# Strassen weight blocks formed by accumulating DMAs, with signs laid out so that they are only added

## The chip, the cores and the metric

One core of a Trainium2 chip runs the program. The metric is the device time of one execution in microseconds (us). The engines are TensorE (PE in the profile, with PEld for its weight loads), VectorE (DVE), ScalarE (ACT), GpSimd (POOL) and SyncE (SP, which here only issues DMAs).

## The reference

One layer of a streaming encoder, 512 tokens by a model width of 2048, all in float32. Nearly all arithmetic is in three projections; between them stand twelve heads of attention of three kinds.

```python
def hybrid_layer(x, norm_g, w_in, b_f, b_gate, qk_norm_g, rel_bias, w_up, w_out):
    hn = rmsnorm(x, norm_g)
    proj = jnp.einsum('bsd,dc->bsc', hn, w_in)          # 2048 -> q, k, v, g of 12 heads, 4 logits, 3 x 2048 gates
    ...
    ya = forgetting_attention(qa, ka, to_heads(br[:, :, 0, 2]), f_logit)
    yb = chunked_relpos_attention(qb, kb, to_heads(br[:, :, 1, 2]), rel_bias)
    yc = stick_breaking_attention(...)
    ys = jnp.stack([from_heads(ya), from_heads(yb), from_heads(yc)], axis=2)
    ys = ys * jax.nn.silu(br[:, :, :, 3])
    up = jnp.einsum('bsnw,nwd->bsnd', ys, w_up)
    merged = jnp.sum(gates * up, axis=2)
    return x + jnp.einsum('bsd,de->bse', merged, w_out)
```

## The kernel before

Tokens lie in the free dimension. A column tile is 128 columns of a weight matrix; its 2048 rows are two halves of 8 k tiles of 128. Each float32 operand is split into a high and a low float32r part (`split_to`: ScalarE writes the high part, VectorE subtracts it from the source, line 93), and `mm3` makes a product of three matmuls: high by high, low of x by high, high of x by low.

Column tiles go in pairs, and a pair is computed by Strassen's method in Winograd's form: the 2 x 2 blocks of the weights (column tile by half of the rows: a11, a12 of the first tile, a21, a22 of the second) and of x (half of the model width by half of the tokens) need seven products of 8 k tiles by 256 tokens in place of eight. Three of the seven stationary operands are blocks as they are (product 1: a11, product 2: a12, product 4: a22), the others are sums: product 5 takes a21 + a22, product 6 that sum less a11, product 7 a11 - a21, product 3 a12 less product 6's operand. `pair_task` makes the seven units of a pair, in the order 1, 2, 6, 7, 4, 5, 3 (for the first pair of the output projection, called late: 1, 2, 5, 3, 6, 7, 4). The sums of x's blocks are made once: `combos` for the input projection (GpSimd, lines 257 to 260, then splits on ScalarE and VectorE), `merged_combos` for the output projection.

Each unit has a load, a preparation (sums and split into `wh` and `wl`), matmuls and an evacuation. Raw weight tiles (`raw`, 512 KB each) rotate through six buffers, `wh` and `wl` through three each, PSUM tiles `acc` through four. All four blocks of a pair are loaded by the unit that comes first in it, on SyncE's queue. The four sums of a pair are VectorE operations on whole raw tiles (lines 315, 324, 325, 327). The loop at the end prepares two units ahead and loads up to seven ahead (`LA`, `LD`); the framework's scheduler then sets the order within each engine's queue, and every engine runs its queue in order. In the first units (`manual_schedule`) TensorE keeps the written order.

The program starts with 16 tiles of x, the first head's q, k, v, g projected from the unnormed x without Strassen's method, and `combos` of the normed x at the same time (`x` there holds x1 and x2, the two halves of the model width; `t` holds t23 and t4, the sums). Then come 46 pairs of the input projection with the attention of the heads between them, the up projections, and eight pairs of the output projection. In the accumulation of a pair's results, `u`, `c1` and `c2` are SBUF tiles that VectorE updates from PSUM after each product.

Of the kernel before, what the change touches and what calls it, by code (L numbers as in the profile page):

```python
# [15 lines left out]
P = 128  # L16
# [9 lines left out]
UK = 8  # L26
# [12 lines left out]
def hybrid_kernel(  # L39
# [60 lines left out]
    def mm3(ps, lh, ll, rh, rl, start, stop):  # L100
        nc.tensor.matmul(ps, lh, rh, start=start, stop=False)  # L101
        nc.tensor.matmul(ps, lh, rl, start=False, stop=False)  # L102
        nc.tensor.matmul(ps, ll, rh, start=False, stop=stop)  # L103

    # ------------------------------------------------------------------ constants
# [18 lines left out]
    class Unit:  # L124
        """A stretch of the tensor engine's work with one stationary operand of up to 8 k tiles."""

        def __init__(self, shape, prep, mms, srcs=(), after=None):
            self.shape, self.prep, self.mms, self.srcs, self.after = shape, prep, mms, srcs, after
            self.hi = self.lo = None
# [4 lines left out]
    def load(u):  # L134
        u.raw = []
        for s, keep in u.srcs:
            t = raw_tile(u.shape)
            nc.sync.dma_start(t, s)
            u.raw.append(t)
            if keep is not None:  # L140
                keep.append(t)
# [8 lines left out]
    def prep_raw(u):  # L150
        split_to(u.hi, u.lo, u.raw[0])
# [21 lines left out]
    # -1 where key k >= j: suffix sums inside a block  # L173
# [4 lines left out]
    # A, rows are queries: NEG where the key (free) is after the query  # L178
# [4 lines left out]
    # C, rows are keys: valid where the query (free) is after the key  # L183
# [7 lines left out]
    # column h has ones on the rows h, 32 + h, 64 + h, 96 + h  # L191
# [6 lines left out]
    # the query gains carry the softmax scale  # L198
# [33 lines left out]
    def rsqrt(y, ps, n):  # L232
        """y = (ps / n + EPS) ** -0.5: a guess by exp and ln, and one Newton step."""
# [64 lines left out]
    def pair_task(src1, src2, ops, done, late=False, before_last=None):  # L298
# [3 lines left out]
        kept = []  # L302
# [608 lines left out]
```

## Time and profile before

| | |
|---|---|
| runs | 1399.37, 1399.85, 1400.12 us (median 1399.85) |
| span of the profiled execution, first to last instruction | 1397.6 us |
| its own time | not listed apart; the runs lie 1.8 to 2.5 us above that span |
| TensorE busy | 1366.3 us, 98% |
| VectorE busy | 1191.8 us, 85% |
| ScalarE busy | 729.7 us, 52% |
| GpSimd busy | 53.7 us, 4% |
| DMA | 176.39 MB, mean 126 GB/s |

The columns of a group of instructions are: line, engine, operation, output and inputs by the program's names, shapes, count, busy us, mean ns of one, and the idle time just before them with what ended it. A row of the order of time has its start, its duration, the engine and line; in brackets stands the idle time ahead of it and who ended it. A row of a stretch has its limits, its length, the busy time (and count) of each engine, TensorE's granted clock as a share of full speed, the DMA engines' mean busy share and GB/s. A line L93 is the helper's, whoever calls it; the tile names tell the calls apart. Matmul rows overlap, since matmuls are pipelined.

### The profile page before, as it was taken

How to read it: one execution, taken by the hardware profiler on the slowest of the kernel's cores; microseconds unless marked ns; L12 is line 12 of the kernel's file. 1: busy time of each engine (PE TensorE's matmuls, PEld its weight loads, DVE VectorE, ACT ScalarE, POOL GpSimd, SP SyncE). 2: the span in 40 equal slices, each digit the busy share in tenths (PEclk: the TensorE clock that was granted, in tenths of full speed). 3: DMA queues.
4: the chain of work that ended last, by engine and by line, in shares of the span. 5: the costliest groups of instructions: out<-in, count | busy, mean ns of one | idle time of the engine just before them, and what ended most of it. 6: DMA issues, size and time to landing. Idle time of an engine off the chain costs nothing.

```text
span 1397.6 us, 25474 instructions
## 1 busy us (share of the span) xinstructions
PE 1366.3 (98%) x10452; PEld 1316.7 (94%) x10452; DVE 1191.8 (85%) x1671; ACT 729.7 (52%) x1042; POOL 53.7 (4%) x60
## 2 busy tenths in 40 slices
PE   6969999999999999999999999999999999999999
PEld 3759999999999999999999999999999988899999
DVE  8999898887978889888888888888888888898886
ACT  6345564544545555555556555545555755453332
POOL 4730000000000000000000000000000000000000
PEclk9989999999999999999999999999999999999999
DMA  7113334323344244342433333333233766535542
GB/s 272 46 46 106 122 102 126 121 91 114 106 129 126 95 114 128 113 129 95 117 122 115 121 94 119 113 114 121 91 115 103 273 197 203 169 109 176 164 151 76
DMA packets 63093, 176.39 MB, mean 126 GB/s; under 512 B 7400, under 2 KB 9320, under 8 KB 62976
## 3 DMA queue, kind: packets, MB, share of 16 engines
q1 hardware_dynamic: 59520, 170.49, 38.4%
q10 hardware_dynamic: 3456, 4.26, 0.8%
q8 instruction: 82, 1.34, 0.4%
q14 instruction: 35, 0.29, 0.1%
HBM read 155.04 MB, written 19.69 MB: 125 GB/s over the span
## 4 chain that ended last, share of the span: by engine, by line
PE 92%; DVE 5%; issue 1%; ACT 0%; POOL 0%; DMA 0%; SPq 0%; DVEq 0%; ACTq 0%; POOLq 0%
PE acc L101 27%; PE acc L103 27%; PE acc L102 27%; PE att L103 3%; PE att L101 3%; PE att L102 3%; DVE x L255 1%; DVE wl L93 1%; PE att L548 1%; PE att L517 1%; PE att L570 1%; DVE x1l L93 1%; PE att L571 1%; PE att L569 1%; DVE t23l L93 0%
## 5 line engine op out<-in xcount | busy, mean ns | idle before, releaser
L92 ACT ACTIVATE wh<-raw 128x1024 fp32r<-128x1024 f32 (+1 forms) x418 | 435.7, 1043 | 549.2 <-PE acc L102 488.2
L93 DVE TENSOR_TENSOR wl<-raw,wh 128x1024 fp32r<-128x1024 f32 (+1 forms) x418 | 503.9, 1206 | 96.7 <-ACT wh L92 95.9
L102 PE MATMUL acc<-x1l,wh 128*128 128x256 f32 (+1 forms) x768 | 222.3, 289 | 10.5 <-DVE x1l L93 10.5
L103 PE MATMUL acc<-x1h,wl 128*128 128x256 f32 (+1 forms) x768 | 222.0, 289 | 2.2 <-DVE wl L93 2.2
L101 PE MATMUL acc<-x1h,wh 128*128 128x256 f32 (+1 forms) x768 | 223.7, 291 | 0.0
L101 PE MATMUL acc<-x2h,wh 128*128 128x256 f32 (+1 forms) x768 | 223.6, 291 | 0.0
L102 PE MATMUL acc<-x2l,wh 128*128 128x256 f32 (+1 forms) x768 | 221.9, 289 | 0.9 <-DVE x2l L93 0.9
L103 PE MATMUL acc<-x2h,wl 128*128 128x256 f32 (+1 forms) x768 | 221.8, 289 | 0.0
L101 PE MATMUL acc<-t23h,wh 128*128 128x256 f32 x736 | 209.7, 285 | 0.0
L103 PE MATMUL acc<-t23h,wl 128*128 128x256 f32 x736 | 208.4, 284 | 0.0
L102 PE MATMUL acc<-t23l,wh 128*128 128x256 f32 x736 | 208.1, 283 | 0.0
L102 PEld LDWEIGHTS acc<-x1l,wh 128*128 128x128 f32 x768 | 147.8, 192 | 13.4 <-DVE x1l L93 11.2
L103 PEld LDWEIGHTS acc<-x1h,wl 128*128 128x128 f32 x768 | 147.8, 193 | 3.9 <-DVE wl L93 2.4
L102 PEld LDWEIGHTS acc<-x2l,wh 128*128 128x128 f32 x768 | 148.0, 193 | 2.4 <-DVE x2l L93 1.1
L101 PEld LDWEIGHTS acc<-x1h,wh 128*128 128x128 f32 x768 | 147.9, 193 | 1.8 <-issue 0.2
L101 PEld LDWEIGHTS acc<-x2h,wh 128*128 128x128 f32 x768 | 148.2, 193 | 1.3
L103 PEld LDWEIGHTS acc<-x2h,wl 128*128 128x128 f32 x768 | 148.0, 193 | 1.3
L101 PEld LDWEIGHTS acc<-t23h,wh 128*128 128x128 f32 x736 | 141.0, 192 | 0.5
L102 PEld LDWEIGHTS acc<-t23l,wh 128*128 128x128 f32 x736 | 141.0, 192 | 0.1
L103 PEld LDWEIGHTS acc<-t23h,wl 128*128 128x128 f32 x736 | 140.7, 191 | 0.3
L101 PE MATMUL acc<-t,wh 128*128 128x256 f32 x368 | 105.1, 286 | 0.0
L102 PE MATMUL acc<-t,wh 128*128 128x256 f32 x368 | 104.4, 284 | 0.0
(256 smaller groups left out, 2728.0 us busy)
## 6 DMA issues: line engine op xcount, KB each, us to landing
raw<-in_w_col SPq DMA_DIRECT2D x192, 512.0 KB, 3.6
raw<-in_w_out SPq DMA_DIRECT2D x32, 512.0 KB, 3.8
gl<-c SPq DMA_DIRECT2D x48, 256.0 KB, 2.0
raw<-in_w_up SPq DMA_DIRECT2D x32, 384.0 KB, 3.2
sg<-gl SPq DMA_DIRECT2D x48, 256.0 KB, 5.0
x<-in_xT SPq DMA_DIRECT2D x16, 256.0 KB, 5.4
xr<-in_xT SPq DMA_DIRECT2D x16, 256.0 KB, 4.4
yd<-y SPq DMA_DIRECT2D x11, 256.0 KB, 2.0
```

What stands on the lines that cost most here:

```text
L92: nc.scalar.activation(hi, src, AF.Copy)
L93: nc.vector.tensor_sub(lo, src, f(hi))
L101: nc.tensor.matmul(ps, lh, rh, start=start, stop=False)
L102: nc.tensor.matmul(ps, lh, rl, start=False, stop=False)
L103: nc.tensor.matmul(ps, ll, rh, start=False, stop=stop)
L255: nc.vector.scalar_tensor_tensor(x, x, gn[:, kt:kt + 1], rstd[0], op0=ALU.mult, op1=ALU.mult)
L517: nc.tensor.transpose(ps[:, blk(i)], st["p"][i][:, blk(j)], identf)
L548: nc.tensor.matmul(ps[:, i * P:], nu_r if i == j else nones_r, part, start=i == j and part is st["lk"][j][0], stop=False)
L569: nc.tensor.matmul(o, vh[:, blk(j)], st["h"][j], start=j == 0, stop=False)
L570: nc.tensor.matmul(o, vl[:, blk(j)], st["h"][j], start=False, stop=False)
L571: nc.tensor.matmul(o, vh[:, blk(j)], st["l"][j], start=False, stop=j == QB - 1)
```

## The change

The signs of the sums are laid out anew, so that every stationary operand is a sum without a minus: product 5 takes a21 + a22, product 6 adds a11 to that, product 3 adds a12 to that, and product 7 takes a11 + a21. For this, x's sum T1 has the other sign in `combos` and `merged_combos`, and the evacuations subtract where they added.

The order of products in a pair is now 5, 1, 2, 6, 7, 4, 3 (the late pair keeps its order). Product 3 accumulates onto product 5's PSUM tile, which stays allocated from the pair's first product to its last; VectorE reads it once between, after product 7. One evacuation a pair is gone.

The sums of raw tiles are made in place by DMAs that GpSimd issues and that add their source to the tile: a22 onto a21's tile, then, once the split for product 5 has read it, a11 onto the same tile (product 6), and after that split a12 (product 3); a21 onto a11's tile after product 1's split (product 7). So a pair has four plain loads (SyncE) and four adding ones (GpSimd), eight reads of 512 KB from HBM for four before. Each plain load is now issued by the unit that needs it. In the late pair VectorE keeps two sums (product 6 and product 3) and two are DMAs.

```diff
     def pair_task(src1, src2, ops, done, late=False, before_last=None):
-        order = (1, 2, 5, 3, 6, 7, 4) if late else (1, 2, 6, 7, 4, 5, 3)
+        order = (1, 2, 5, 3, 6, 7, 4) if late else (5, 1, 2, 6, 7, 4, 3)
+        (a11, a12), (a21, a22) = src1, src2
+        def add(t, src):
+            nc.gpsimd.dma_start(t, src, accum_op=ALU.add)
+        def load_of(i):
+            def go(u):
+                p = order[i]
+                if p in (1, 2, 4, 5):
+                    w[p] = raw_tile()
+                    nc.sync.dma_start(w[p], {1: a11, 2: a12, 4: a22, 5: a21}[p])
+                if p == 5:
+                    add(w[5], a22)
+            return go
         def prep_of(i):
             def go(u):
-                if i == 0:
-                    w[1], a21, w[4], w[2] = kept
-                    split_to(u.hi, u.lo, w[1])
-                    w[5] = raw_tile()
-                    nc.vector.tensor_add(w[5], a21, w[4])
...
-                split_to(u.hi, u.lo, w[p])
-                if i == 1:
-                    if not late:
-                        nc.vector.tensor_sub(w[7], w[1], w[7])
-                        nc.vector.tensor_sub(w[6], w[5], w[1])
-                if i == (1 if late else 4):
-                    nc.vector.tensor_sub(w[3], w[3], w[6])
+                split_to(u.hi, u.lo, w[p])
+                if late and p == 5:
+                    w[6], w[3] = raw_tile(), w[5]
+                    nc.vector.tensor_add(w[6], w[5], w[1])
+                    nc.vector.tensor_add(w[3], w[6], w[2])
+                    w[7] = w[1]
+                    add(w[7], a21)
+                elif late:
+                    return
+                elif p == 5:
+                    w[6] = w[5]
+                    add(w[6], a11)
+                elif p == 1:
+                    w[7] = w[1]
+                    add(w[7], a21)
+                elif p == 6:
+                    w[3] = w[6]
+                    add(w[3], a12)
         def mms_of(i):
-                st["ps"] = ps = acc()[:, LH]
+                st[p] = ps = st[5] if p == 3 else acc()[:, LH]
                 for j in range(UK):
-                    mm3(ps, u.hi[:, j, :], u.lo[:, j, :], *ops[order[i]](j), j == 0, j == UK - 1)
+                    mm3(ps, u.hi[:, j, :], u.lo[:, j, :], *ops[p](j), j == 0 and p != 3, j == UK - 1, p == 3)
         def after_of(i):
                 elif p == 7:
-                    add(u[:, RH], u[:, LH], ps)
+                    sub(u[:, RH], u[:, LH], ps)
+                    sub(c2[:, RH], u[:, RH], c2[:, RH] if late else st[5])
-                elif p == 5:
-                    add(c2[:, RH], u[:, RH], ps)
-                    add(u[:, LH], u[:, LH], ps)
...
+                elif p == 3:
+                    sub(c1[:, RH], ps, u[:, LH])
```

In the start of the program, VectorE's queue had, ahead of the first splits of the normed x1 (`x1l`), the following rows. The first pair's raw tiles are 453 (a11), 455 (a21), 457 (a22) and 459 (a12); `wl` is the low part of a weight split, `t23l` that of x's sums, `c` a scaled result of the first head.

```order
L315 TENSOR_TENSOR raw_667<-raw_455,raw_457 128x1024
L626 TENSOR_TENSOR c_539<-acc_378,rstd_362 128x512
L324 TENSOR_TENSOR raw_455<-raw_453,raw_455 128x1024
L93 TENSOR_TENSOR t23l_168<-t_122_501,t23h_167 128x512
L93 TENSOR_TENSOR wl_619<-raw_407,wh_618 128x1024
L93 TENSOR_TENSOR t_9_140<-t_123_502,t_9_140 128x256
L93 TENSOR_TENSOR x1l_146<-x_81,x1h_145 128x512
```

At the same place it now has these:

```order
L641 TENSOR_TENSOR c_536<-acc_378,rstd_362 128x512
L93 TENSOR_TENSOR t23l_168<-t_119_496,t23h_167 128x512
L93 TENSOR_TENSOR wl_618<-raw_407,wh_617 128x1024
L93 TENSOR_TENSOR t_9_140<-t_120_497,t_9_140 128x256
L93 TENSOR_TENSOR x1l_146<-x_81,x1h_145 128x512
```

Lines 315 and 324 are gone from there; so are 325 and 327, which stood further on between the splits of x1 and x2.

GpSimd's queue, in the same stretch, made the last two k tiles of x's sums like this (x_207 and x_209 become x1, x_225 and x_227 belong to x2):

```order
L257 TENSOR_TENSOR t_134_596<-x_225,x_207 128x256
L258 TENSOR_TENSOR x_207<-x_207 128x256
L259 TENSOR_TENSOR t_134_596<-x_225,x_207 128x256
L260 TENSOR_TENSOR t_135_597<-t_134_596,x_225 128x256
L257 TENSOR_TENSOR t_136_608<-x_227,x_209 128x256
L258 TENSOR_TENSOR x_209<-x_209 128x256
```

Now adding DMAs (line 312) stand among them: the one on raw_453 adds a11 onto the first pair's a21 + a22, and ahead of the rows of x_203 stands one on raw_782, for the second pair.

```order
L256 TENSOR_TENSOR t_133_595<-x_225,x_207 128x256
L312 DMA raw_453<-in_w_col 128x1024
L257 TENSOR_TENSOR x_207<-x_207 128x256
L258 TENSOR_TENSOR t_133_595<-x_225,x_207 128x256
L259 TENSOR_TENSOR t_134_596<-t_133_595,x_225 128x256
L256 TENSOR_TENSOR t_135_607<-x_227,x_209 128x256
L257 TENSOR_TENSOR x_209<-x_209 128x256
L312 DMA raw_510<-in_w_col 128x1024
```

Two issues now precede the row that makes x_209 which did not before; the add on raw_510 (a21 onto a11) follows it.

More of the change, by code (lines that the diff above doesn't have):

```diff
@@ L134, in load @@
     def load(u):
[L135 to L141, printed above, removed]
+        if u.load is not None:
+            u.load(u)
+        elif u.src is not None:
+            u.raw = raw_tile(u.shape)
+            nc.sync.dma_start(u.raw, u.src)
     def prep(u):
@@ L150, in prep_raw @@
     def prep_raw(u):
-        split_to(u.hi, u.lo, u.raw[0])
+        split_to(u.hi, u.lo, u.raw)
     for kt in range(4):
@@ L373, in after_of @@
             return go
-        src = {0: [(src1[0], kept), (src2[0], kept), (src2[1], kept), (src1[1], kept)]}
-        return [Unit([UK, P], prep_of(i), mms_of(i), srcs=src.get(i, ()), after=after_of(i)) for i in range(7)]
+        return [Unit([UK, P], prep_of(i), mms_of(i), load=load_of(i), after=after_of(i)) for i in range(7)]
     side = {}
@@ L795, in hybrid_kernel, with rest @@
     for e in range(0, DT, 2):
-        def rest(c1l, c1r, c2, e=e):
-            for c, i, sl in ((c2, 1, slice(0, S)), (c1l, 0, LH), (c1r, 0, RH)):
+        def rest(c1l, v, c2, e=e):
+            for c, i, sl in ((c2, 1, slice(0, S)), (c1l, 0, LH), (v, 0, RH)):
                 if i == 1 or sl is LH:
```

46 lines of the change are left out of this document (19 added, 27 removed).

## The prediction

> **What bounds the kernel now.** I read the page's busy shares first, then the stretches, then TensorE's own waits, and last the order of time on VectorE and GpSimd in the one stretch that has waits.
>
> ```profile
> span 1397.6 us, 25474 instructions
> PE 1366.3 (98%) x10452; PEld 1316.7 (94%) x10452; DVE 1191.8 (85%) x1671; ACT 729.7 (52%) x1042; POOL 53.7 (4%) x60
> ```
>
> TensorE is busy 98% of the span, so all that any change off TensorE can win lies in the 31 us it is idle. The stretches say where (TensorE, weight loads, VectorE, ScalarE, GpSimd; granted clock; DMA share; GB/s):
>
> ```profile
> 0.00:20.00 20.00, 7.74 (x15) 1.14 (x15) 15.89 (x27) 12.40 (x19) 11.20 (x23) 1.00 0.93 350
> 60.00:80.00 20.00, 15.02 (x73) 12.31 (x72) 20.00 (x18) 12.19 (x21) 18.44 (x16) 1.00 0.09 28
> 80.00:100.00 20.00, 11.36 (x68) 10.87 (x69) 19.93 (x34) 9.76 (x17) 3.43 (x4) 0.66 0.21 57
> 89.00:95.00 6.00, 5.12 (x24) 4.92 (x24) 6.00 (x11) 1.33 (x2) 0.00 (x0) 0.60 0.04 5
> 100.00:120.00 20.00, 20.00 (x165) 19.87 (x164) 17.32 (x34) 8.80 (x15) 0.00 (x0) 1.00 0.41 130
> 200.00:400.00 200.00, 200.00 (x1654) 199.33 (x1653) 170.08 (x233) 99.44 (x142) 0.00 (x0) 1.00 0.36 110
> 1200.00:1300.00 100.00, 97.98 (x693) 92.03 (x691) 89.35 (x127) 46.89 (x64) 0.00 (x0) 1.00 0.45 150
> 1300.00:1360.00 60.00, 60.00 (x503) 60.00 (x501) 50.08 (x63) 22.63 (x25) 0.00 (x0) 1.00 0.50 155
> ```
>
> From 100 us on TensorE never rests (200.00 of 200) although VectorE is at 85%: there VectorE's load is hidden and relieving it wins nothing. From 60 to 95 it is the other way round: VectorE is busy without a gap and TensorE waits. About 12 us of the idle time lie before 20 us, under the loading of x, which the change leaves alone. TensorE's waits by name, at the start and where the up projections end:
>
> ```profile
> 81.47 0.58 PE L102 MATMUL acc<-x1l,wh 128*128 128x256 f32 x1 [4.18 <-DVE x1l L93]
> 88.75 0.58 PE L102 MATMUL acc<-x1l,wh 128*128 128x256 f32 x1 [6.27 <-DVE x1l L93]
> 95.02 0.39 PE L102 MATMUL acc<-x2l,wh 128*128 128x256 f32 x1 [0.90 <-DVE x2l L93]
> PE acc L103 <- DVE wl L93: 1.0, 2, 0.8
> PE acc L101 <- ACT wh L92: 1.0, 2, 0.6
> ```
>
> These are the first pair's products 1 and 2, fed one k tile at a time by VectorE; after 95.02 the pair runs through. In the VectorE rows ahead of that, four of the removed sums stand in the queue:
>
> ```profile
> 59.38 1.76 DVE L315 TENSOR_TENSOR raw<-raw,raw 128x1024 f32<-128x1024 f32 x1
> 61.67 1.21 DVE L324 TENSOR_TENSOR raw<-raw,raw 128x1024 f32<-128x1024 f32 x1
> 75.39 1.22 DVE L93 TENSOR_TENSOR x1l<-x,x1h 128x512 fp32r<-128x512 f32 x1
> 77.68 1.74 DVE L325 TENSOR_TENSOR raw<-raw,raw 128x1024 f32<-128x1024 f32 x1
> 84.74 1.21 DVE L327 TENSOR_TENSOR raw<-raw,raw 128x1024 f32<-128x1024 f32 x1
> 88.02 0.68 DVE L93 TENSOR_TENSOR x1l<-x,x1h 128x512 fp32r<-128x512 f32 x1
> 94.30 0.67 DVE L93 TENSOR_TENSOR x2l<-x,x2h 128x512 fp32r<-128x512 f32 x1
> ```
>
> The same subtraction takes 1.22 us at 75 and 0.68 at 88: until 83.7 GpSimd forms the sums of x beside it, and the two slow each other.
>
> ```profile
> 73.47 1.71 POOL L257 TENSOR_TENSOR t<-x,x 128x256 f32<-128x256 f32 x1
> 80.08 0.78 POOL L258 TENSOR_TENSOR x<-x 128x256 f32<-128x256 f32 x1
> 82.08 1.59 POOL L260 TENSOR_TENSOR t<-t,x 128x256 f32<-128x256 f32 x1
> 80.90 0.63 ACT L92 ACTIVATE x1h<-x 128x512 fp32r<-128x512 f32 x1 [0.84 <-POOL x L258]
> ```
>
> **The change, part by part.**
>
> *Sums off VectorE.* Four operations per pair go:
>
> ```profile
> L315 DVE TENSOR_TENSOR raw<-raw,raw 128x1024 f32<-128x1024 f32 x54 | 66.6, 1233 | 1.8 <-DMA raw<-in_w_out 0.7
> L324 DVE TENSOR_TENSOR raw<-raw,raw 128x1024 f32<-128x1024 f32 x53 | 64.3, 1214 | 0.0
> L364 DVE TENSOR_TENSOR u<-u,acc 128x256 f32<-128x256 f32 x53 | 22.0, 414 | 0.0
> ```
>
> Four at about 1.22 us and one evacuation of 0.414 us (product 3 now adds onto product 5's bank) are 5.3 us a pair, 280 us over 53 pairs; the late pair keeps two sums. From 100 to 1200 us this is worth nothing (above). At the start the four removed rows add up to 5.9 us.
>
> *GpSimd gets the adds.* Two of them stand ahead of x's last k tile on its queue (the order in the section on the change). No row shows GpSimd issuing a DMA. An issue on SP's queue costs 0.43 us; the longest of the sums that GpSimd forms here took 2.59:
>
> ```profile
> 2.66 0.43 SPq L138 DMA_DIRECT2D raw<-in_w_col  x1
> 52.05 2.59 POOL L257 TENSOR_TENSOR t<-x,x 128x256 f32<-128x256 f32 x1 [6.02 <-DVE t L93]
> ```
>
> Those are my ends. I take 1.1, near GpSimd's shorter rows (0.78 to 1.71), since it is the same engine working by program. The Trainium skill (DMA: Bandwidth & Descriptors, "Latency and other measured facts") puts the first byte of a GpSimd DMA at about 1 us; no row here shows it, and the sum by it would be the same.
>
> *The start, step by step.* VectorE alone would bring the last x1 tile 5.9 us sooner, from 88.0 to 82.1. But GpSimd's row that makes it started at 80.08 and now starts two issues (2.2) later and ends at 83.1; ScalarE's copy (0.63) makes 83.7, and VectorE's in-order queue, which now meets GpSimd's tiles 6 and 7 as they come, costs another 1.3 by walking both orders with these durations: 85.0, a gain of 3.0. With an issue at 0.43 I get 84, at 2.59 about 88. The rows from there to the last x2 tile took 6.3 before (88.0 to 94.3), so that is at 91.3 plus 0.7. TensorE now has products 5 and 1 to do on x1 before it needs x2: at 85.7, 3 + 24 + 21 = 48 matmuls. Before, it came out of this wait at a granted clock of 0.60 and did 24 in 5.12 us (0.21 each), and ran at full clock after 95, where 165 take 20 us (0.121). I take the slow pace for the first 25 and the full one for 23: 5.3 + 2.8, so 93.8. That is after x2 (92.0), so x2 no longer matters. Then remain 3 matmuls and four products, 99 x 0.121 = 12.0: the pair ends at 105.8. Before it was 95.02 + (3 + 5 x 24) x 0.121 = 109.9. Gain 4.1 us. Bounds: 1.5 (issue 2.59, or the slow clock held throughout), 7.0 (GpSimd in nobody's way: x1 at 82.1).
>
> *After the up projections.* VectorE's sums leave the queue ahead of the first weight splits of the output projection, where TensorE's waits on weight splits sum to 2.0 us (the last two of the rows of waits above). I take 0.8, since two of the late pair's four sums stay; ends 0 and 2.0.
>
> *Each sum now waits for a DMA.* Per pair, split of product 5, add onto the same tile, split of product 6, add, split of product 3. A split is 1.04 us on ScalarE and 1.21 on VectorE, 2.25:
>
> ```profile
> L92 ACT ACTIVATE wh<-raw 128x1024 fp32r<-128x1024 f32 (+1 forms) x418 | 435.7, 1043 | 549.2 <-PE acc L102 488.2 <-PE att L102 23.9 <-issue 21.5
> L93 DVE TENSOR_TENSOR wl<-raw,wh 128x1024 fp32r<-128x1024 f32 (+1 forms) x418 | 503.9, 1206 | 96.7 <-ACT wh L92 95.9
> raw<-in_w_col SPq DMA_DIRECT2D x192, 512.0 KB, 3.6
> x<-in_xT SPq DMA_DIRECT2D x16, 256.0 KB, 5.4
> 564.34 0.33 PE att L517 x3
> 651.15 0.33 PE att L517 x3
> ```
>
> A product lasts 24 x 0.121 = 2.9 us, and `wh` has three buffers, so a split may begin two products (5.8) ahead. Product 5 is split 3.55 before it runs; product 3, sixth after it, must be split by 17.4. Between them lie two adds and two splits: 17.4 + 3.55 = 2L + 4.5, so each add may take L = 8.2 us from split to landed sum before TensorE waits. ScalarE sits 488 us waiting for TensorE to free `wh`: that is the cover. My L: a plain load's 3.6, plus 1.4 for reading 512 KB a second time at the 376 GB/s of the loading of x (350 at a share of 0.93), plus 1.1 for GpSimd: 6.1. Ends: 3.6, and twice a load plus 2.6, 9.8. At 6.1 steady state costs nothing. What queues behind: on GpSimd the next pair's first add stands ahead of this pair's second, and on ScalarE and VectorE a late split holds all evacuations.
>
> *DMA load.* A head (four pairs) takes 86.8 us (564.34 to 651.15), a pair 21.7; its weights, 2.1 MB, are 97 GB/s of the 110 that make a share of 0.36. Read twice: 0.36 + 0.32 = 0.68. In the output projection 155 + 103 GB/s, 0.83. Both hold.
>
> *Signs, one PSUM bank held through the pair, the last product's order:* nothing; three `acc` buffers rotate and each evacuation is done two products ahead of need; the tail after the last product is one VectorE row and one store as before.
>
> **Sum.** 1397.6 - 4.1 - 0.8 = 1392.7 for the profiled execution; the runs' median is 1399.85, 2.25 above that span, so 1394.9.
>
> **The rivals.**
>
> *Hidden after all (no change within 0.2%, 2.8 us, which is about what timing can tell here).* GpSimd paces the start: it is busy 18.44 of 20 us from 60 to 80, and the adds come on top. At 2.59 an issue the start gains 1.5 and the sum is 1397 to 1399. Against it: GpSimd idles after 83.7 while VectorE had 11 us of backlog.
>
> *An add takes more than 8.2 us (slower).* One mechanism: the chain of two adds in a pair becomes longer than six products. It decides at L = 8.2; beyond, each pair loses 2(L - 8.2). At 8.6 that is 0.8 x 53 = 42 us, 1437; at my upper end of 9.8, 170 us, 1565. For it: x's small loads took 5.4 us when many were in flight, and now adds overlap loads. Against: shares of 0.36 leave room.
>
> *The adds fill the DMA engines (slower).* If an added byte costs two plain ones, a head's share becomes 0.36 + 2 x 0.32 = 1.0 and the output projection's 0.50 + 0.66 = 1.16, which over its 162 us is 26 us: 1421. By the burst rate of 376 GB/s the same traffic is (155 + 206)/376 = 0.96, and nothing is lost. So this decides near twice the cost, and I price it at 0 to 26. The Trainium skill states it as a rule (Collectives: The Full Stack, "The bandwidth ceiling: the fold count and why AG ≠ RS ≠ AR"): an adding transfer reads two sources through one ring and runs at half the rate. No run here shows that yet; by that rule the time would be up to the 1421 worked out above.
>
> *More than forecast.* If GpSimd's issues are free the start gives 7.0, and 2.0 at the up projections: 1391.
>
> **How the numbers follow.** Forecast and its better version (1391 to 1397) 0.55; hidden 0.17; chain too long 0.16; engines full 0.12. Predicted: 1394.9, the likeliest. The low end is 1391, the better version; the high end 1430 takes in full engines and the beginnings of a long chain, and leaves out the rest of that, about 0.14. The likeliest case's own range is 1391 to 1398. Faster by over 0.2%: 0.55; within: 0.17; slower: 0.28.
>
> **What would show it.** Right: VectorE near 65% with TensorE still 20.00 of 20 from 110 on; the first pair's wait for the last x1 tile ending near 85 and no wait for x2; add landings of 5 to 8 us. Wrong: rows in which ScalarE's `wh` waits for a DMA on `raw` and TensorE for `wh`, every pair again; a DMA share near 1; GpSimd rows late between 60 and 85.

## The result, and the profile after

The changed kernel takes 1452.24 us (median of four runs, 1440.49 to 1453.02), the kernel before 1399.98 in the same session: a ratio of 1.035, 95% interval 1.032 to 1.039. It is slower by 52 us where the forecast said faster by 5, and it lies above the range.

The page of the changed kernel, first its busy shares, then the two DMA queues that move the weights (q0: what GpSimd issues; q1: what the others issue; packets, MB, share of 16 engines' span), then the issues with their median time to landing:

```profile
span 1451.3 us, 25979 instructions
...
PE 1388.3 (96%) x10452; PEld 1327.2 (91%) x10452; DVE 945.0 (65%) x1403; ACT 725.0 (50%) x1045; POOL 236.1 (16%) x274
...
q0 software_dynamic: 30816, 112.21, 44.6%
q1 hardware_dynamic: 59520, 170.49, 34.4%
...
raw<-in_w_col SPq DMA_DIRECT2D x192, 512.0 KB, 4.5
raw<-in_w_col POOLq DMA_DIRECT2D x184, 512.0 KB, 6.8
...
raw<-in_w_out POOLq DMA_DIRECT2D x30, 512.0 KB, 7.3
```

VectorE went from 85% to 65%, as forecast, and TensorE's span did not shrink. The two queue rows hold the main number of this case. The adds are 112.21 MB and keep the 16 engines busy for 44.6% of 1451.3 us, 5.77 us for each MB; the plain loads and all other transfers of q1 take 34.4% for 170.49 MB, 2.93 us for each MB. By these two rows an added byte costs 1.97 plain ones of the other queue; against a plain copy on its own queue it costs 1.76 (`plain_copy`, below). The Trainium skill (Collectives: The Full Stack, "The bandwidth ceiling: the fold count and why AG ≠ RS ≠ AR") has 1.93 as the measured ratio between gathering and reducing in a ring of four ranks, and puts it down to the add's two source reads. The trace comes near that size; the reason is one that no run here shows.

Where TensorE lost time, by stretch (TensorE, weight loads, VectorE, ScalarE, GpSimd, granted clock, DMA share, GB/s):

```profile
80.00:100.00 20.00, 13.64 (x93) 13.15 (x94) 18.89 (x29) 10.36 (x18) 4.98 (x5) 0.74 0.45 92
200.00:400.00 200.00, 196.44 (x1593) 195.09 (x1592) 123.66 (x179) 96.50 (x139) 30.31 (x35) 0.98 0.85 198
400.00:600.00 200.00, 194.58 (x1585) 191.81 (x1584) 122.50 (x188) 101.70 (x145) 31.21 (x36) 1.00 0.85 205
1300.00:1360.00 60.00, 56.53 (x459) 55.11 (x458) 32.33 (x44) 21.56 (x23) 10.54 (x12) 1.00 0.93 232
```

Before, TensorE was busy 200.00 of 200 us with 1654 matmuls from 200 to 400, and 60.00 of 60 with 503 in the output projection from 1300. Now it makes 1593 and 459. The DMA share is 0.85 and 0.93, where it was 0.36 and 0.50. The start, on the other hand, is faster: 93 matmuls from 80 to 100 us instead of 68.

The waits say what is late (who waited, for whom, us in total, times, longest):

```profile
DVE wl L93 <- ACT wh L92: 321.7, 228, 5.6
ACT wh L92 <- DMA raw<-in_w_col: 201.0, 85, 5.2
...
ACT wh L92 <- DMA raw<-in_w_out: 63.1, 19, 7.3
...
PE acc L104 <- DVE wl L93: 17.1, 21, 1.9
```

Before, ScalarE's splits waited for TensorE to free `wh`, which was the cover the forecast counted on. Now 104 of the 418 splits wait for a weight tile to land, VectorE waits for them, and TensorE now and then for VectorE.

One pair in the steady state. GpSimd's rows in order of time:

```profile
563.12 0.86 POOL L312 DMA_DIRECT2D raw<-in_w_col  x1 [9.02 <-DVE u L375]
565.06 0.86 POOL L312 DMA_DIRECT2D raw<-in_w_col  x1 [1.07 <-DVE mx L520]
567.86 0.86 POOL L312 DMA_DIRECT2D raw<-in_w_col  x1 [1.94 <-DVE sm L522]
```

The chain that ended last, at the same place (start, length, what):

```profile
565.06 8.10 DMA raw<-in_w_col
573.25 1.06 ACT wh L92
```

The add at 563.12 is that for the next pair's product 5; it stands ahead of this pair's adds for product 6 (565.06) and product 7 (567.86). Three adds lie within 5 us of each other. The one that is needed first, product 6's, is second in the queue and takes 8.10 us from its issue to its landing; the split that waits for it starts at 573.25.

### The profile page after: what moved, and what is told of

It is laid out like the page before. It is cut to its first block, busy times and chain, and to the rows that moved or that the text cites. A ratio compares the mean times of both kernels' runs of the same rounds, so it can differ in the third digit from the quotient of the medians.

```text
span 1451.3 us, 25979 instructions
## 1 busy us (share of the span) xinstructions
PE 1388.3 (96%) x10452; PEld 1327.2 (91%) x10452; DVE 945.0 (65%) x1403; ACT 725.0 (50%) x1045; POOL 236.1 (16%) x274
## 3 DMA queue, kind: packets, MB, share of 16 engines
q0 software_dynamic: 30816, 112.21, 44.6%
q1 hardware_dynamic: 59520, 170.49, 34.4%
## 4 chain that ended last, share of the span: by engine, by line
PE 53%; DMA 24%; DVE 10%; issue 6%; ACT 5%; POOL 1%; SPq 0%; POOLq 0%; ACTq 0%; DVEq 0%
DMA raw<-in_w_col 17%; PE acc L104 14%; PE acc L102 14%; PE acc L103 14%; DMA raw<-in_w_out 6%; DVE wl L93 4%; ACT wh L92 3%; PE att L103 2%; PE att L104 2%; PE att L102 2%; PE att L563 1%; DVE x L254 1%; POOL raw L312 1%; PE att L532 1%; DVE x1l L93 0%
## 5 line engine op out<-in xcount | busy, mean ns | idle before, releaser
L312 POOL DMA_DIRECT2D raw<-in_w_col x184 | 160.2, 881 | 883.1 <-DVE wl L93 359.1
L102 PE MATMUL acc<-t,wh 128*128 128x256 f32 x368 | 105.5, 287 | 0.0
```

The lines of the kernel that those rows point to most:

```text
L102: nc.tensor.matmul(ps, lh, rh, start=start, stop=False, skip_group_check=more)
L312: nc.gpsimd.dma_start(t, src, accum_op=ALU.add)
```

## The experiments

The kernel before ran beside every kernel; its medians were 1399.98 to 1400.47, so differences below are against 1400. The questions, in turn: is it the adding; which queue or order makes adds late; what of signs, accumulator and product order costs anything by itself; and is the gain at the start real.

### Is it the adding?

`plain_copy` issues the same DMAs from the same queue at the same places, but lets them overwrite. It leaves out the sums.

```diff
-            nc.gpsimd.dma_start(t, src, accum_op=ALU.add)
+            nc.gpsimd.dma_start(t, src)
```

> The changed kernel with the same DMAs on the same queue, with the same waits, but each of them overwrites its tile instead of adding to it (the sums of weight blocks are left out). Theory A (an adding DMA occupies the engines about twice as long as a copy, 44.6% of the span for 112 MB against 34.4% for 170 MB, and this makes the chain split, add, split, add, split of a pair longer than its products): their share falls to 22 to 25%, the landing from 6.8 us to 4.5 to 5.5, waits of wh for raw vanish, time 1394 to 1402 us. Rival B (what costs is that GpSimd issues them, or the waits as such, whatever the transfer does): landing and time stay, 1435 to 1455 us.

It took 1400.86 us, ratio 1.000 (0.999 to 1.001). The q0 row and the issue row of its page:

```profile
q0 software_dynamic: 30816, 112.21, 26.3%
...
raw<-in_w_col POOLq DMA_DIRECT2D x184, 512.0 KB, 4.5
```

Two of its stretches:

```profile
400.00:600.00 200.00, 200.00 (x1650) 199.03 (x1649) 128.28 (x192) 106.09 (x148) 19.53 (x37) 1.00 0.69 213
1300.00:1360.00 60.00, 60.00 (x502) 60.00 (x501) 36.77 (x48) 22.82 (x24) 6.34 (x12) 1.00 0.78 257
```

The same queue, waits, order and bytes land in 4.5 us instead of 6.8, the same 112.21 MB take 26.3% instead of 44.6%, and TensorE does not rest in these stretches. So the 52 us are the price of adding. The DMA share here, 0.69 and 0.78, is close to what the forecast had for the changed kernel (0.68 and 0.83): it had counted the bytes and not their price. The run shows a second thing: with VectorE at 68% and TensorE without a rest, the main stretch makes 1650 matmuls in 200 us, where the kernel before made 1647. Taking work off VectorE is worth nothing there. (The whole time says less: this kernel makes 175 matmuls from 60 to 100 us, where the kernel before makes 141, and loses that again later.)

### Which adds are late, and where?

`pool_order` keeps the adds and only makes GpSimd's queue follow the order in which the program writes them, so that a pair's own adds go ahead of the next pair's first.

```diff
         if i == OFF["man"]:
             order.close()
+            order.enter_context(tc.manual_schedule(engines={mybir.EngineType.Pool}))
```

> The changed kernel with GpSimd's queue held to another order from the second pair on: a pair's own adds (products 6, 7, 3) come ahead of the next pair's first add (product 5), which the scheduler had put in front of them. Same transfers and bytes. Theory A1 (the chain is late because the add for product 6 stands behind the next pair's first add, some 2.5 us of engine time): its wait shrinks by about 2.5 us, and the time falls to 1400 to 1425 us. Rival A2 (the engines are simply full, DMA share 0.85 whatever the order): 1438 to 1455 us as now.

1425.86 us, ratio 1.018 (1.016 to 1.020): half of the loss, 26.4 us, is gone by the order of one queue alone. The adds onto column weights land in 5.9 us at the median instead of 6.8. Its stretches:

```profile
400.00:600.00 200.00, 199.93 (x1648) 198.79 (x1647) 128.72 (x194) 104.60 (x148) 32.22 (x37) 1.00 0.86 211
600.00:800.00 200.00, 195.96 (x1592) 192.83 (x1591) 125.81 (x192) 109.22 (x157) 32.81 (x39) 1.00 0.83 206
1300.00:1360.00 60.00, 56.88 (x463) 55.85 (x464) 34.19 (x48) 20.45 (x22) 8.68 (x10) 1.00 0.96 242
```

From 400 to 600 us TensorE is whole again with the DMA engines as busy as before (0.86); from 600 to 800 it still loses 4 us, to late splits and to reads of the shared accumulator. The output projection is not whole.

`after_out` goes the other way: the changed kernel with the output projection's eight pairs alone as in the kernel before (sums on VectorE, an accumulator for each product, the old product order), with the new signs.

```diff
-            units.extend(pair_task(out_col(e), out_col(e + 1), mops, both, late=True))
+            units.extend(pair_old(out_col(e), out_col(e + 1), mops, both, late=True))
-            units.extend(pair_task(out_col(e), out_col(e + 1), mops, last, before_last=rest))
+            units.extend(pair_old(out_col(e), out_col(e + 1), mops, last, before_last=rest))
```

> The changed kernel with the output projection's eight pairs alone as in the kernel before (sums on VectorE, own accumulators, old product order; the new signs). If the parts stand each for itself: 1452.2 - 18.3 = 1434 us, range 1430 to 1438, TensorE at 80.0 of 80 in the last 80 us before the end and the main stretch at 194 to 197 of 200 as in the changed kernel. If the output projection only pays for what GpSimd's queue brings late: 1445 or more.

1430.73 us, ratio 1.021 (1.019 to 1.023): 21.5 us less than the changed kernel. Two of its stretches:

```profile
400.00:600.00 200.00, 195.67 (x1601) 193.55 (x1600) 123.80 (x190) 102.01 (x146) 31.12 (x36) 1.00 0.87 208
1300.00:1360.00 60.00, 60.00 (x503) 60.00 (x502) 50.83 (x65) 22.60 (x25) 0.00 (x0) 1.00 0.51 159
```

Now the projection is whole and the main stretch is as in the changed kernel. The two parts stand each for itself: 21.5 us here, 18.3 in the next pair of kernels.

`adds_main` takes both together, and gives product 3 an accumulator of its own (next section): all sums of the main stretch by adding DMAs in written order, those of the output projection on VectorE.

```diff
+        order = (5, 1, 2, 6, 7, 4, 3) if early else (1, 2, 5, 3, 6, 7, 4) if late else (1, 2, 6, 7, 4, 5, 3)
...
-        units.extend(pair_task(gate_col(n, d), gate_col(n, d + 1), ops, done, late))
+        units.extend(pair_task(gate_col(n, d), gate_col(n, d + 1), ops, done, late, early=True))
...
-        units.extend(pair_task(col(n, Q, h), col(n, K, h), ops, done_qk))
+        units.extend(pair_task(col(n, Q, h), col(n, K, h), ops, done_qk, early=True))
...
         if i == OFF["man"]:
             order.close()
+            order.enter_context(tc.manual_schedule(engines={mybir.EngineType.Pool}))
```

Pairs with `early` have their sums by adding DMAs; the others, those of the output projection, have them on VectorE.

> pool_own (all sums by accumulating DMA, own accumulators, adds in written order on GpSimd's queue; 1420.3 us) with the output projection's eight pairs as in old_order, their sums on VectorE. If the output projection makes the 12 us between pool_own and own_bank: 1406 to 1411 us, TensorE 80.0 of 80 busy from 1300 to 1380. If the adds cost it in the main stretch: 1415 to 1421.

1402.06 us, ratio 1.002 (1.001 to 1.003), below the range expected for it. `pool_own`, which differs in the output projection alone, took 1420.34. A stretch of `pool_own`'s output projection:

```profile
1300.00:1340.00 40.00, 37.51 (x289) 37.09 (x288) 21.33 (x28) 14.13 (x17) 6.52 (x8) 0.91 0.91 223
```

The same of `adds_main`, and one of its main stretch:

```profile
400.00:600.00 200.00, 200.00 (x1646) 198.91 (x1645) 131.79 (x203) 110.40 (x162) 32.21 (x38) 1.00 0.87 214
...
1300.00:1340.00 40.00, 40.00 (x336) 40.00 (x335) 33.30 (x42) 15.08 (x17) 0.00 (x0) 1.00 0.51 155
```

With a DMA share of 0.87 the stretch from 400 to 600 us loses nothing (this profile is of the fastest of the ten runs, 1399.69 us); the engines' load alone is no loss there. In the output projection the adds are one. A pair there is 168 matmuls, and 336 take 40 us, so TensorE wants a pair every 20.0 us. Four adds of 512 KB at 5.77 us an MB are 12.1 us of all engines, four plain loads at 2.93 are 6.1, and residual and output, 1.05 MB at the same price, 3.1: an estimate of 21.3 us. That is more than there is, and over eight pairs it is 10 of the 18.3 us. Whether full engines alone set the pace there is not shown: a pair's own chain of three splits and two adds (see the part on why the prediction was wrong) comes to about 20.5 us in the projection of `pool_order`, also more than 20.0. In the main stretch a pair has 21.7 us, since attention stands between, and less besides the weights to move.

### What do the signs, the accumulator and the product order cost?

`signs_dve` has the new signs, order and shared accumulator, with all sums on VectorE and the loads as before. `chain_dve` makes the sums for products 6 and 3 on VectorE and leaves two adds a pair to DMAs.

The edit of `signs_dve`, without the late pair and without its loads, which all stand in a pair's first unit as before the change:

```diff
+                if i == 0:
+                    w[5] = raw_tile()
+                    nc.vector.tensor_add(w[5], w[7], w[4])
+                    nc.vector.tensor_add(w[7], w[7], w[1])
...
                 elif p == 5:
                     w[6] = w[5]
-                    add(w[6], a11)
...
+                    nc.vector.tensor_add(w[6], w[5], w[1])
                 elif p == 6:
                     w[3] = w[6]
-                    add(w[3], a12)
+                    nc.vector.tensor_add(w[3], w[6], w[2])
```

The edit of `chain_dve`:

```diff
-                elif p == 5:
+                elif p == 1:
                     w[6] = w[5]
-                    add(w[6], a11)
-                elif p == 1:
+                    nc.vector.tensor_add(w[6], w[5], w[1])
                     w[7] = w[1]
                     add(w[7], a21)
                 elif p == 6:
                     w[3] = w[6]
-                    add(w[3], a12)
+                    nc.vector.tensor_add(w[3], w[6], w[2])
```

> Only the other half of the change: the new signs, the order 5, 1, 2, 6, 7, 4, 3 and product 3 accumulating onto product 5's PSUM bank, but all four sums on VectorE and no adding DMA; loads as before the change. Theory A: the loss is all in the DMAs, so 1396 to 1400 us, and up to 3 us under the kernel before, since the first pair has two products on x1 to do before it needs x2. Rival D (holding a PSUM bank through the pair or the new order costs TensorE waits in every pair): above 1410 us.

> Half of the change: VectorE forms the two sums that hang on one another in a pair (products 6 and 3), DMAs add the other two (products 5 and 7). Adds per pair 2 in place of 4, plain loads as in the changed kernel. Theory A: no add waits for a split that waits for an add, and the DMA share falls from 0.85 to about 0.6, so TensorE no longer waits: 1394 to 1400 us, with part of the gain at the start kept. Rival C (adding DMAs slow the other transfers or the splits as such): half of the loss stays, 1418 to 1430 us.

They took 1415.41 (ratio 1.011, 1.010 to 1.013) and 1414.77 (1.011, 1.009 to 1.012); a single further run of `chain_dve`, labelled chain_man, gave 1411.41. I had expected `signs_dve` near the kernel before, and `chain_dve` lies between the two ranges named for it. All of `signs_dve`'s loss lies before 400 us, at the stick-breaking heads. TensorE's row for the first head's suffix sums in `signs_dve` (they read lkh, the high part of that head's tile lk):

```profile
129.36 0.78 PE L561 MATMUL att<-lkh,nu_r 128*128 128x512 f32 x3 [4.40 <-ACT lkh L92]
```

The same in the kernel before, without a wait:

```profile
135.11 0.56 PE L548 MATMUL att<-lkh,nu_r 128*128 128x512 f32 x2
```

In the kernel before, the scheduler set them behind 552 products' matmuls, in `signs_dve` behind 480. I took this order to be the cause (theory P) and had TensorE's queue keep the written order through the whole program.

```diff
-        if i == OFF["man"]:
-            order.close()
         cur[0] = i
...
+    order.close()
```

`signs_man` is `signs_dve` with this edit, `after_man` the changed kernel with it, `before_man` the kernel before with it. `after_both` is `after_man` with GpSimd's queue in written order as well.

> New signs, product order and shared accumulator with every weight sum on VectorE, as in the run signs_dve (1415.4 us), but TensorE's queue keeps the order in which the program writes its matmuls through all units (before it did so for the first 17 units only). In signs_dve the first head's suffix-sum matmuls stand 72 product matmuls earlier on TensorE than in the kernel before (after 480 of them, not 552), and the later heads' last two score tiles stand together; TensorE waits there for lkh (10.3 us). Theory P (the loss of about 15 us of signs_dve is this order on TensorE alone): 1394 to 1400 us, no wait of TensorE on lkh, 200.0 us of 200 busy from 200 to 400 us. Rival S (the shared accumulator and the signs themselves cost it: a PSUM buffer held through the pair, sums of weights late): 1410 us or more, TensorE still waits between 120 and 400 us.

> The changed kernel with TensorE's queue in the written order through all units and nothing else. If the order on TensorE (about 15 us by signs_dve) and the adds that come late (theory A) add up: 1452 - 15 = 1437 us, range 1425 to 1445, with ScalarE's splits still waiting on raw from the column weights. If the order on TensorE is nothing once the adds are late (they wait in its shadow): 1448 to 1455. If the late adds matter only through that order: under 1410.

> The changed kernel with the written order kept on TensorE and on GpSimd's DMA queue alike (pair's own adds ahead of the next pair's). pool_order alone gave 1425.9. Theory: both losses are queue orders, so 1425.9 - 15 = 1411 us, range 1402 to 1418, what is left lying in the output projection (DMA share .95) and the up projections. Rival (the DMA engines' load costs time of its own in the main stretch): 1418 or more, with TensorE below 199 us of 200 busy in the stretches from 400 to 1000 us.

> The kernel before with TensorE's queue in the written order through all units. If the written order costs by itself (signs_man: TensorE waited 35.9 us in 13 times on the accumulator shared with product 3, and 29.8 us in 8 times on ScalarE's rv of the query and key norms): the waits on rv stay, those on the accumulator go, 1425 to 1450 us. If only the shared accumulator made the written order bad: 1398 to 1405.

Theory P fell. `signs_man` took 1483.74 us, `after_man` 1506.07, `after_both` 1479.6, and even the kernel before takes 1424.92 in the written order (a single run). There it waits for the softmax tiles `p` (11.1 us in 4 times), not for `rv` as I had thought. The scheduler's order is the better one in all of them. But `signs_man` showed what the scheduler had been filling. The sum of one of TensorE's waits in it:

```profile
PE acc L102 <- DVE c L374: 35.9, 13, 3.6
```

One case of it in the order of time, VectorE's rows and then TensorE's:

```profile
463.37 1.22 DVE L93 TENSOR_TENSOR wl<-raw,wh 128x1024 fp32r<-128x1024 f32 x1
464.50 0.69 DVE L93 TENSOR_TENSOR qkl<-rs,qkh 128x512 fp32r<-128x512 f32 x1
465.11 0.41 DVE L374 TENSOR_TENSOR c<-u,acc 128x256 f32<-128x256 f32 x1
...
465.67 0.35 PE L102 MATMUL acc<-x2h,wh 128*128 128x256 f32 x1 [3.55 <-DVE c L374]
```

Line 374 is the read of product 5's bank after product 7. Product 3 adds onto that bank, and may not begin until the read is done. Only product 4, 2.9 us, lies between; VectorE had the query and key norms to do first.

So `own_bank`, `chain_own` and `pool_own` give product 3 an accumulator of its own, in `signs_dve`, `chain_dve` and `pool_order`: ScalarE copies product 5 out when it ends, and VectorE makes one more subtraction. (In these three the residual is missing from the right half of seven of the sixteen output tiles; the instructions are the same.)

```diff
-                st[p] = ps = st[5] if p == 3 else acc()[:, LH]
+                st[p] = ps = acc()[:, LH]
...
                     if late:
                         sub(c1[:, RH], c1[:, RH], u[:, LH])
+                    else:
+                        sub(c1[:, RH], c2[:, RH], u[:, LH])
...
-                elif p == 5 and late:
+                elif p == 5:
                     nc.scalar.activation(c2[:, RH], ps, AF.Copy)
```

> signs_dve (1415.4 us: new signs and order, sums on VectorE) with an accumulator of its own for product 3: product 5 is copied to SBUF by ScalarE when it ends, and one more VectorE subtraction of 128x256 makes up for the sum on the bank. Theory S (the shared accumulator: product 3 may not start on the bank until VectorE has read product 5 from it, which happens only one product earlier; the run signs_man waited there 35.9 us in 13 times, and in signs_dve the scheduler filled the same places with attention matmuls that came too early): 1395 to 1402 us, no wait of TensorE on lkh above 3 us, 200.0 of 200 busy from 200 to 400 us. Rival O (the order 5,1,2,6,7,4,3 or the signs place the attention early, whatever the bank): 1408 us or more.

> chain_dve (1414.8 us: w5 and w7 by accumulating DMA, w6 and w3 on VectorE) with the own accumulator for product 3. Theory S: its early loss goes as in own_bank, and the half load of adds (q0 at 24 per cent) costs nothing in the main stretch: 1394 to 1400 us, the best of the versions, since the earlier start (some 3.5 us) is kept. Rival O: 1410 or more.

> The changed kernel with all adds by DMA, in the written order on GpSimd's queue (pool_order, 1425.9 us), and the own accumulator for product 3. Theory S: the 12 to 15 us of the accumulator go, what stays is the output projection and the end (about 8 us by the busy time of pool_order from 1200 us) and the adds that are still late: 1404 to 1416. If the accumulator is hidden here by late adds: 1420 or more.

They took 1409.48, 1407.95 and 1420.34 us: 5.9, 6.8 and 5.5 us less than their pairs. The shared accumulator costs about 6 us in each, less than I expected of it: all three times lie above the ranges of theory S. And `own_bank` still waits on lkh. Its rows at the second head, VectorE and then TensorE:

```profile
189.85 1.22 DVE L343 TENSOR_TENSOR raw<-raw,raw 128x1024 f32<-128x1024 f32 x1
190.99 0.55 DVE L551 SCALAR_TENSOR_TENSOR lk<-z,lk 128x384 f32<-128x384 f32 x1
...
197.29 0.68 PE L563 MATMUL att<-lkh,nu_r 128*128 128x512 f32 x2 [1.55 <-ACT lkh L92]
```

VectorE in the kernel before, at the same step of that head:

```profile
190.29 1.15 DVE L93 TENSOR_TENSOR lkl<-lk,lkh 128x384 fp32r<-128x384 f32 x2
191.36 1.22 DVE L315 TENSOR_TENSOR raw<-raw,raw 128x1024 f32<-128x1024 f32 x1
```

In the kernel before, the first sum of weights (L315) comes after the head's last lk tiles are split. In the new product order a sum (L343, for product 3) stands among the steps of lk. `old_order` tests that: the new signs, with the product order, the places of the sums and the accumulators of the kernel before.

```diff
+        order = (5, 1, 2, 6, 7, 4, 3) if early else (1, 2, 5, 3, 6, 7, 4) if late else (1, 2, 6, 7, 4, 5, 3)
...
+                if i == 0:
+                    w[5] = raw_tile()
+                    nc.vector.tensor_add(w[5], w[7], w[4])
+                if i == (0 if late else 1):
+                    nc.vector.tensor_add(w[7], w[1], w[7])
+                    w[6], w[3] = w[1], w[2]
+                    nc.vector.tensor_add(w[6], w[5], w[1])
+                if i == (1 if late else 4):
+                    nc.vector.tensor_add(w[3], w[3], w[6])
```

Here no pair is `early`.

> The new signs with everything else as in the kernel before: products in the order 1, 2, 6, 7, 4, 5, 3, each on its own accumulator, the three groups of sums on VectorE behind the splits of the products 1, 2 and 4 of a pair, all as sums instead of differences. TensorE's order has the first head's suffix-sum matmuls after 552 product matmuls again. Theory Q (what own_bank still lost, 9.3 us, is the product order 5,1,2,6,7,4,3, which puts VectorE's sums among the steps of the attention's lk tiles): 1398.5 to 1402, no wait of TensorE on lkh. Rival (the signs themselves or the combined operands cost it): 1406 or more.

1400.06 us, ratio 1.000 (0.999 to 1.001). The signs cost nothing; the product order with VectorE's sums at its places costs 9.4 us (`own_bank` less `old_order`; the extra copy and subtraction of `own_bank` are in it).

### Is the gain at the start real?

`first_one` and `first_two` are `old_order` with the changed kernel's form (product 5 first, adds by DMA, but own accumulators) in the first one or two pairs.

```diff
-        units.extend(pair_task(gate_col(n, d), gate_col(n, d + 1), ops, done, late))
+        units.extend(pair_task(gate_col(n, d), gate_col(n, d + 1), ops, done, late,
+                               early=len(units) < 17))
```

This is `first_one`; `first_two` has 24 in place of 17.

> old_order, with the changed kernel's form (product 5 first, four accumulating DMAs, but an accumulator of its own for product 3) for the first Strassen pair alone. Forecast of the prediction's start: about 4 us by 100 us (3.5 us measured in the changed kernel's trace). Theory: the start is won and nothing is lost later, 1395 to 1398.5 us. Rival (the gain is given back in the following attention stage): 1399 to 1402.

> old_order with the changed kernel's form for the first two Strassen pairs. The scheduler places the first head's suffix sums after 504 product matmuls here, not 552. If that place costs a wait on lkh as in own_bank: 1398 to 1404 us; if VectorE, freed of the sums of two pairs, has lkh ready in time: 1395 to 1398.

`first_one` took 1398.06 us, ratio 0.9986 (0.9977 to 0.9995), the only version that beats the kernel before; `first_two` 1401.57, ratio 1.0008 (0.9999 to 1.0017). In `first_one` the start is won:

```profile
60.00:80.00 20.00, 15.91 (x77) 13.12 (x76) 18.36 (x17) 11.86 (x21) 18.00 (x19) 0.98 0.25 55
80.00:100.00 20.00, 13.81 (x96) 13.23 (x96) 19.88 (x31) 10.57 (x18) 3.49 (x4) 0.76 0.46 103
```

Part of it is given back:

```profile
121.93 0.38 PE L102 MATMUL acc<-t,wh 128*128 128x256 f32 x1 [1.61 <-ACT u L367]
```

It makes 77 + 96 = 173 matmuls from 60 to 100 us, the kernel before 141: 32 x 0.121 = 3.9 us ahead. The wait of 1.61 us at 121.93 takes 1.6 of that; 1.9 arrive at the end. In `first_two` the suffix sums stand behind 504 products' matmuls, and there is a wait on lkh of 2.3 us; from 100 to 200 us it makes 788 matmuls where `old_order` makes 822, 4.1 us, so all of the start is given back.

### The sum

| step | us | change |
|---|---|---|
| changed kernel | 1452.2 | |
| GpSimd's queue in written order (`pool_order`) | 1425.9 | -26.4 |
| own accumulator for product 3 (`pool_own`) | 1420.3 | -5.5 |
| output projection's sums on VectorE (`adds_main`) | 1402.1 | -18.3 |
| kernel before | 1400.0 | |

The last step also gives the output projection back its old product order. That part is free: `signs_dve`, with the new order and all sums on VectorE, keeps TensorE busy for 60.00 of 60 us from 1300. What the last 2.1 us are made of, the gain at the start against the new product order, was not taken apart further.

## Why the prediction was wrong

*"VectorE's load is hidden and relieving it wins nothing": right.* `plain_copy`, at 68%, makes no more matmuls from 400 to 600 us than the kernel before.

*The start: right in kind and nearly in size.* The forecast had the wait for the last x1 tile end at 85.7, none of weight for x2, and a gain of 4.1. The changed kernel's rows:

```profile
86.32 0.58 PE L103 MATMUL acc<-x1l,wh 128*128 128x256 f32 x1 [3.57 <-DVE x1l L93]
...
92.26 0.39 PE L104 MATMUL acc<-x2h,wl 128*128 128x256 f32 x1 [0.62 <-DVE wl L93]
```

From 60 to 100 us it makes 170 matmuls against 141, 3.5 us. An issue on GpSimd took 0.86 (I took 1.1). What the step lacked is what follows: the next stage gives some of it back, and `first_one` keeps 1.9.

*"Each sum now waits for a DMA", L = 6.1 against the 8.2 allowed: this step failed, on both sides.* An add took 6.8 us from its issue to its landing at the median (the 0.86 of the issue is in it), inside the 5 to 8 us that the forecast named as a sign of being right. Counted as the forecast counts L, from the end of the split to the landed sum, 43 pairs of the input projection show 8.0 us on the mean for product 6's add and 6.2 for product 3's. In none of them do the two together reach twice 8.2. Yet the split for product 6 starts within 0.2 us of the landing in 37 of the 43, in `plain_copy` in one. So 8.2 was too much to allow. The pair at 560 goes on like this (VectorE's, GpSimd's and ScalarE's rows, in the order of time):

```profile
563.54 1.22 DVE L93 TENSOR_TENSOR wl<-raw,wh 128x1024 fp32r<-128x1024 f32 x1
...
574.34 1.23 DVE L93 TENSOR_TENSOR wl<-raw,wh 128x1024 fp32r<-128x1024 f32 x1 [2.35 <-ACT wh L92]
...
575.86 0.86 POOL L312 DMA_DIRECT2D raw<-in_w_col  x1 [7.13 <-DVE mx L520]
...
581.66 1.06 ACT L92 ACTIVATE wh<-raw 128x1024 fp32r<-128x1024 f32 x1 [1.28 <-PE att L532]
582.75 1.23 DVE L93 TENSOR_TENSOR wl<-raw,wh 128x1024 fp32r<-128x1024 f32 x1 [0.25 <-ACT wh L92]
...
584.38 1.06 ACT L92 ACTIVATE wh<-raw 128x1024 fp32r<-128x1024 f32 x1 [1.38 <-PE acc L103]
```

These are the end of product 5's split, the end of product 6's, the add for product 3, product 3's split, and the start of the next pair's split for product 5. That last one stands behind product 3's split in the same queues. So three splits of 2.3 us and two adds have to fit into one pair's time, and with the forecast's 21.7 us that leaves 7.4 for each add (an estimate from these rows). The forecast gave product 5's split a start two products early in every pair, though the split ahead of it was allowed to end as late as the start of product 3. Measured from the start of product 5's split to the end of product 3's, the chain took 22.6 us on the mean, and the pairs came every 22.8 us, in `plain_copy` every 22.0.

What made L too small is what the forecast named and gave no price: "the next pair's first add stands ahead of this pair's second". In `pool_order` the two adds take 6.0 and 6.1 on the mean, the forecast's own size, the chain 20.6, and 26.4 us of the loss are gone. The rival with this mechanism was priced at 42 us for L = 8.6, and had 0.16; by its condition, L over 8.2, a mean of 7.1 would not have set it off.

*"Both hold" (DMA shares of 0.68 and 0.83): failed.* The shares were 0.85 and 0.93. The step counted twice the bytes; an added byte costs 1.97 plain ones, about as the rival of the full engines had it. In the main stretch a share of 0.87 still holds (`adds_main`). The adds of the output projection cost 18.3 to 21.5 us, against 26 in that rival's working; how much of it is the engines' load is open.

*"Signs, one PSUM bank held through the pair, the last product's order: nothing": one of three right.* Signs: nothing. The bank: 5.5 to 6.8 us. The forecast counted its buffers ("three `acc` buffers rotate"), not the wait that it adds: product 3 behind VectorE's read. That price was measured where VectorE makes sums or adds come late; in `plain_copy`, with neither, TensorE rests nowhere from 400 to 600 us, shared bank and all. The product order: up to 9.4 us where VectorE keeps the sums.

*After the up projections, 0.8:* no run tells it apart.

*The range.* The two slow rivals were given as alternatives, with a chance each. Both grow with the price of an added byte, and here both came, in different parts of the kernel, so their costs add: 1400 + 26 + 18 + 6 is 1450, and the range ended at 1430, short of it.

## What to carry to other kernels

Taking work off an engine that does not set the pace wins nothing there, and the price is paid where it lands: here the sums moved from a hidden engine to transfers at 1.76 times the cost of a copy. Before moving sums into adding DMAs, work out for each stage the engines' time per unit of work (5.77 us per added MB, 2.93 per plain one here) against the time that TensorE leaves, add up the whole chain that one unit sends through an in-order queue, not only the part behind its first step, and put each queue's issues in the order in which they are needed. When a matmul group adds onto a bank that another engine reads in between, that read can become a wait for TensorE, whatever the number of banks.

## What the hardware showed beyond that

A wait of TensorE can cost more than its length. After the 3.55 us at 465.67 in `signs_man`, three matmuls take 0.64 us instead of 0.36 until about 469.5. Two matmul starts three apart, then a shorter wait of the same trace with the stretch behind it (granted clock 0.50):

```profile
467.36 0.41 PE L102 MATMUL acc<-x2h,wh 128*128 128x256 f32 x1
...
468.00 0.41 PE L102 MATMUL acc<-x2h,wh 128*128 128x256 f32 x1
```

```profile
188.35 0.35 PE L102 MATMUL acc<-x2h,wh 128*128 128x256 f32 x1 [2.39 <-DVE c L374]
...
189.63:193.04 3.41, 3.41 (x18) 3.31 (x17) 1.82 (x5) 1.51 (x4) 0.00 (x0) 0.50 0.51 189
```

Some 16 matmuls at 0.21 instead of 0.12 are another 1.5 us, so the longer wait cost about 5. The wait of 1.61 us in `first_one` left the pace as it was. The Trainium skill (TensorE: Matmul & The Clock Gate, "The HAM clock gate (the "warmup" mystery)") has the clock halve after an idle window of about 3.4 us and come back after a busy one as long. The 3.4 us at half pace agree; the 2.39 us do not, a shorter wait was enough here.

Written by GpSimd's queue without adding, 512 KB landed in 4.5 us and cost 26.3% of 1400 us for 112.21 MB, 3.28 us an MB; adding takes 1.76 times that on the same queue.
